# Value products of the samples in four column tiles, forget sums in four column tiles, and the samples' spatial weights turned once by VectorE

## The chip, the cores and the metric

One core of a Trainium2 chip runs the whole kernel. The metric is the time of one execution on the device in microseconds (us); less is better. The engines of the core each run their own instructions in order: TensorE (PE, with its weight loads listed apart as PEld), VectorE (DVE), ScalarE (ACT), GpSimd (POOL), and SyncE (SP), which issues most of the DMAs. They wait for one another through semaphores.

## What is computed

A trunk of two layers, for a prompt of 512 frames and eight samples of 16 frames each, 640 rows in all, with 1024 model channels, all in float32. Layer 0 mixes by spatial gating in blocks of 128 frames; layer 1 is attention with forget gates, over 16 heads of 128 channels. Each layer ends with an output product, two norms and a gated embedding. The parts that the change touches:

```python
# layer 0: a 128x128 matrix of spatial weights per group of 128 channels;
# samples use the first 16x16 of it (n = 16)
wm = jnp.where(chunk_causal_mask(n)[None], w_s[:, :n, :n], 0.0).astype(v.dtype)
s = jnp.einsum('gij,bnjgc->bnigc', wm, vb) + b_s[:, :n].T[None, None, :, :, None].astype(v.dtype)
# layer 1: running sums of the log forget values, and attention with them as a bias
cT = jnp.cumsum(logf, axis=1).transpose(0, 2, 1)
s = s + ci[..., :, None] - cT[:, :, None, :]
# layer 1, samples: 256 cached rows and 16 new ones
v = jnp.concatenate([v_cache.astype(v_new.dtype), v_new], axis=1)
p = jax.nn.softmax(s, axis=-1).astype(v.dtype)
return jnp.einsum('bhqk,bkhd->bqhd', p, v).reshape(B, T, H * dh)
```

## The kernel before, in words

**Products.** The large projections are made as three reduced-precision products of a high and a low part (`mm3`, L272 to L274). In both layers most of them run in a scheme of seven products instead of eight (`seven_products`): twelve matmuls of 128x320 for each of the seven, into four PSUM banks in turn (tiles named `pb`). ACT writes the high part of the weights (L289, L292) and DVE the low part (L290, L293); POOL makes the sums of weight blocks that the scheme wants (L211); DVE adds up the seven results (L713, L724, L726, L729). The small products are plain float32 matmuls, which leave two records each in the trace; transposes on PE leave one.

**Layer 0.** The groups of 128 channels are worked in pairs, eight pairs in all. Between the two projections of a pair, `spatial_weights` prepares two matrices for each of its groups. For the prompt it turns the 128x128 weights with PE (L688), and ACT copies them out with their mask (L690, L691). For the samples, DVE spreads the 16x16 weights along a block diagonal (L684) into the one buffer `ax`, PE turns that (L689), and ACT copies it out (L692). The 16x16 weights of all groups, `w16`, are gathered at the start of the layer by eight DMAs, one for each sample's 16 partitions. After the pair's projections, `gate_spatial` uses the matrices (L745 for the prompt, L746 for the samples). In the first three pairs a panel of layer norm is added (`layer_norm_panel`).

**Layer 1.** First the values, keys and queries of head pair 0 are projected. Meanwhile the logits of the forget gates are made in column tiles (L968: four matmuls with 32 output rows each, in four groups of 32 columns of PE), and from them the log forget values `lft`. `forget_sums` then makes the running sums for the prompt: four matmuls with the triangle of ones `tri`, for heads in 16 output rows and up to 512 columns (L1006). ACT copies them out, they are stored in `c_sc`, and `load_w0` reads one head's row back onto all 128 partitions when that head is due. The same routine makes the samples' sums (L1014 to L1016).

Then follow eight head pairs. For each, the projections of the next pair run on PE, and the attention of this pair is put between them: `interleave` gives each piece a time, and a scheduler turns the whole into an order for each engine. For the prompt a piece is scores, turn (transposes, L1186) or values (L1193). For the samples (`sample_pieces`, twice a pair, for four sequences each) the scores are eight matmuls of 32 output rows in column tiles (L1243). In `values`, one full-width matmul brings in the new rows of all four sequences (L1267), and eight of 32 output rows the cached ones (L1270), in four column groups. The last pair's attention stands between the output products of layer 1.

Of the kernel before, what the change touches and what calls it, by code (L numbers as in the profile page):

```python
# [17 lines left out]
F32 = mybir.dt.float32  # L18
# [39 lines left out]
def hybrid_trunk(tc, x_prompt, x_sample, ck, cv, clf, p_prompt, p_sample, norm_pre, norm_post,  # L58
# [27 lines left out]
    c_sc = dram.tile([H, SEQ], F32, name="c_sc")  # L86
# [579 lines left out]
    assert o_A + 256 <= o_X  # L666
    for b in range(NB):
        dma(w16[b * TS:(b + 1) * TS], w_s[0, :, :TS, :TS].rearrange("g i j -> i g j"))
# [11 lines left out]
    def spatial_weights(g):  # L680
        z = g % 2
        raw, wm, ws, ax = r1(o_wsr + z * P, P), r1(o_wm + z * P, P), r1(o_ws + z * P, P), r1(o_ax, P)
        nc.vector.scalar_tensor_tensor(out=spb[z], in0=spb[z], scalar=lnb[:, g:g + 1], in1=r1(o_bs + z * P, P), op0=ALU.mult, op1=ALU.add)
        nc.vector.tensor_tensor(  # L684
            out=ax.rearrange("p (b j) -> p b j", b=NB), in0=blk.rearrange("p (b j) -> p b j", b=NB),
            in1=w16[:, g:g + 1, :].broadcast_to([P, NB, TS]), op=ALU.mult)
        b = bank(SPA)
        nc.tensor.transpose(out=b[:, :P], in_=raw, identity=ident)  # L688
        nc.tensor.transpose(out=b[:, P:2 * P], in_=ax, identity=ident)  # L689
        nc.scalar.activation(out=wm[0:64, :], in_=b[0:64, 0:P], func=AF.Copy)  # L690
        nc.scalar.activation(out=wm[64:128, 64:128], in_=b[64:128, 64:P], func=AF.Copy)  # L691
        nc.scalar.activation(out=ws, in_=b[:, P:2 * P], func=AF.Copy)  # L692
# [263 lines left out]
    cT, ex, cS = r1(o_PT + 288, SEQ, H), r1(o_PT + 800, P), r1(o_V + 1760, 272)  # L956
# [46 lines left out]
    def forget_sums():  # L1003
        pb = bank(ATT)
        for t in range(4):
            nc.tensor.matmul(pb[:H, t * P:], lf3[:, t], tri[:, :SEQ - t * P], start=(t == 0), stop=(t == 3))  # L1006
        nc.scalar.activation(out=cT, in_=pb[:H, :], func=AF.Copy)
# [128 lines left out]
    def load_w0(h, queue=None):  # L1136
        dma(w0_of(h), c_sc[h].partition_broadcast(P), queue)
# [92 lines left out]
    def sample_pieces(p, bg):  # L1230
# [34 lines left out]
        def values():  # L1265
            O = bank(ATT)
            nc.tensor.matmul(O[:, :256], pt[:, 256:], v_of(p)[:, 4], start=True, stop=False)  # L1267
            for t in range(2):
                for bl in range(4):
                    nc.tensor.matmul(O[32 * bl:32 * bl + 32, :256], pt[:, t * P + 32 * bl:t * P + 32 * bl + 32],  # L1270
                                     vv[:, bl, t], start=False, stop=(t == 1))
# [136 lines left out]
```

## Time and profile before

| | |
|---|---|
| time, median of 3 runs | 1280.55 us (1275.15, 1280.55, 1281.59) |
| time of the profiled execution | 1274.95 us |
| its span, first to last instruction | 1273.1 us |
| mean granted clock of PE | 0.999 |
| layer 0, spatial pairs | about 127 to 345 us |
| forget sums | 566.2 to 568.5 us |
| attention of pairs 0 to 6 beside projections | about 581 to 1061 us |

The profile is that of one execution. Its page gives busy times, the chain of work that ended last, and groups of instructions by line. A row of a group has the line, the engine, the operation, what is written and read, the count, the busy time, the mean of one instruction, and the idle time before it with the engine that ended it. A row of the timeline has the start (us from the start of the span), the duration, the engine, line and operation, and how many records were merged into it. A row of the stages gives the busy time of PE, PEld, DVE, ACT and POOL in that order, each with its count, and then the granted clock, the DMA share and GB/s. Line numbers are those of the kernel before.

### The profile page before, as it was taken

The page shows a single profiled execution, that of the slowest core. Times are in us where ns is not written, and L with a number is a line of the kernel's source. Part 1 is how long each engine was busy: PE and PEld are TensorE (multiplying, and loading weights), DVE is VectorE, ACT ScalarE, POOL GpSimd, SP SyncE. Part 2 cuts the span into 40 slices and gives each one's busy share as a digit, 9 for nine tenths or more (in the row PEclk, how much of TensorE's full clock was granted, in tenths as well). Part 3 has the DMA queues.
Part 4 walks back from the last instruction along what each step waited for, and adds up shares of the span by engine and source line. Part 5 has one row for each costly group of instructions (what it writes and reads, how often), then busy time and mean ns, then how long its engine had stood idle before and what let it go on. Part 6 is the DMA issues. An engine that isn't in the chain of part 4 may idle for free.

```text
span 1273.1 us, 21241 instructions
## 1 busy us (share of the span) xinstructions
PE 1265.6 (99%) x7942; PEld 1138.3 (89%) x7942; DVE 957.5 (75%) x1795; ACT 595.3 (47%) x1076; POOL 353.3 (28%) x323
## 2 busy tenths in 40 slices
PE   9999999999999999999999999999999999999998
PEld 7888999999988888889999999999999999788887
DVE  6844999999943374799888898989888988545643
ACT  5424555444445253565445444545454545455331
POOL 1012445454000010155444434444435430000100
PEclk9999999999999999999999999999999999999999
DMA  5532343323324212658898758777888759632211
GB/s 204 177 102 67 112 125 120 92 88 98 121 85 161 88 35 87 150 125 174 159 169 169 185 150 187 164 164 143 152 162 179 178 114 287 221 129 83 67 66 50
DMA packets 275544, 171.52 MB, mean 135 GB/s; under 512 B 188721, under 2 KB 238689, under 8 KB 275442
## 3 DMA queue, kind: packets, MB, share of 16 engines
q1 hardware_dynamic: 261170, 127.80, 36.6%
q0 software_dynamic: 9760, 36.05, 14.0%
q10 hardware_dynamic: 4512, 6.33, 1.5%
q8 instruction: 62, 1.02, 0.3%
q14 instruction: 40, 0.33, 0.1%
HBM read 148.55 MB, written 21.59 MB: 134 GB/s over the span
## 4 chain that ended last, share of the span: by engine, by line
PE 98%; DVE 2%; DMA 0%; issue 0%; ACT 0%
PE pb L272 27%; PE pb L274 27%; PE pb L273 27%; PE pb L1193 3%; PE pb L419 2%; PE pb L1270 2%; PE pb L1186 1%; PE pb L1243 1%; PE pb L745 1%; PE pb L317 1%; PE pb L1058 1%; PE pb L1071 1%; PE pb L1267 1%; DVE W L290 0%; PE pb L1262 0%; PE pb L1059 0%
## 5 line engine op out<-in xcount | busy, mean ns | idle before, releaser
L272 PE MATMUL pb<-A,W 128*128 128x320 f32 (+1 forms) x752 | 240.8, 320 | 0.0
L273 PE MATMUL pb<-A,W 128*128 128x320 f32 (+1 forms) x752 | 233.8, 311 | 0.0
L274 PE MATMUL pb<-A,W 128*128 128x320 f32 (+1 forms) x752 | 233.3, 310 | 0.0
L290 DVE TENSOR_TENSOR W<-RAW,W 128x1024 fp32r<-128x1024 f32 (+1 forms) x122 | 146.1, 1198 | 73.0 <-ACT W L289 71.0
L273 PE MATMUL pb<-W,A 128*128 128x512 f32 x498 | 194.6, 391 | 0.0
L272 PE MATMUL pb<-W,A 128*128 128x512 f32 x498 | 194.6, 393 | 0.0
L274 PE MATMUL pb<-W,A 128*128 128x512 f32 x498 | 193.8, 392 | 0.0
L289 ACT ACTIVATE W<-RAW 128x1024 fp32r<-128x1024 f32 (+1 forms) x122 | 115.8, 949 | 87.9 <-PE pb L274 43.0
L272 PEld LDWEIGHTS pb<-A,W 128*128 128x128 f32 x752 | 141.7, 188 | 1.0 <-issue 0.2
L273 PEld LDWEIGHTS pb<-A,W 128*128 128x128 f32 x752 | 141.7, 188 | 0.5
L274 PEld LDWEIGHTS pb<-A,W 128*128 128x128 f32 x752 | 141.2, 188 | 0.0
L272 PE MATMUL pb<-tbf,W 128*128 128x320 f32 x360 | 119.0, 330 | 0.4 <-DVE R L1099 0.4
L303 POOL TENSOR_TENSOR SML<-SML 128x1 f32<-128x1 f32 x20 | 15.5, 777 | 349.8 <-DVE SML L301 345.0
L274 PE MATMUL pb<-tbf,W 128*128 128x320 f32 x360 | 111.4, 309 | 0.0
L273 PE MATMUL pb<-tbf,W 128*128 128x320 f32 x360 | 111.2, 309 | 0.0
L274 PEld LDWEIGHTS pb<-W,A 128*128 128x128 f32 x498 | 93.4, 188 | 19.3 <-issue 0.4
L273 PEld LDWEIGHTS pb<-W,A 128*128 128x128 f32 x498 | 93.6, 188 | 18.8
L272 PEld LDWEIGHTS pb<-W,A 128*128 128x128 f32 x498 | 93.5, 188 | 18.6
L211 POOL TENSOR_TENSOR sff<-RAW 128x512 f32<-128x512 f32 x46 | 60.9, 1324 | 177.4 <-DVE W L290 114.6
L713 DVE TENSOR_TENSOR R<-R,pb 128x320 f32<-128x320 f32 x184 | 86.5, 478 | 15.0 <-PE pb L274 13.7
L290 DVE TENSOR_TENSOR A<-R,A 128x640 fp32r<-128x640 f32 (+1 forms) x42 | 35.5, 880 | 57.6 <-ACT A L289 57.2
L272 PEld LDWEIGHTS pb<-tbf,W 128*128 128x128 f32 x360 | 67.8, 188 | 10.4 <-issue 6.6
(272 smaller groups left out, 2848.6 us busy)
## 6 DMA issues: line engine op xcount, KB each, us to landing
RAW<-in_fox_w_in POOLq DMA_DIRECT2D x46, 512.0 KB, 7.1
RAW<-in_gmlp_w_in SPq DMA_DIRECT2D x40, 512.0 KB
R<-in_cache_fox_k SPq DMA_DIRECT2D x128, 128.0 KB
R<-in_cache_fox_v SPq DMA_DIRECT2D x32, 512.0 KB
RAW<-in_gmlp_w_out SPq DMA_DIRECT2D x16, 512.0 KB
RAW<-in_ple_w_gate SPq DMA_DIRECT2D x16, 512.0 KB
RAW<-in_fox_w_out SPq DMA_DIRECT2D x16, 512.0 KB
R<-in_fox_w_in POOLq DMA_DIRECT2D x14, 512.0 KB, 7.8
```

Source lines behind the costliest of these rows:

```text
L211: nc.gpsimd.tensor_tensor(out=o, in0=a, in1=b, op=op)
L272: nc.tensor.matmul(out, lh, rh, start=start, stop=False)
L273: nc.tensor.matmul(out, lh, rl, start=False, stop=False)
L274: nc.tensor.matmul(out, ll, rh, start=False, stop=stop)
L289: first = nc.scalar.activation(out=hi, in_=src, func=AF.Copy)
L290: nc.vector.tensor_tensor(out=lo, in0=src, in1=f(hi), op=ALU.subtract)
L303: behind["pool"] = nc.gpsimd.tensor_tensor(out=q, in0=t, in1=mhalf, op=ALU.pow)
L317: behind["pe"] = nc.tensor.transpose(out=b[:, j * P:(j + 1) * P], in_=src[:, (4 * c + j) * P:(4 * c + j + 1) * P], identity=ident)
L419: line[e] = make(*args, **kw)
L713: behind["dve"] = nc.vector.tensor_tensor(out=into(i, j), in0=a, in1=b, op=ALU.add)
L1193: nc.tensor.matmul(O[:, d], v[:, j, hh * P:(hh + 1) * P], pt[:, j * P:(j + 1) * P], start=(j == 0), stop=(j == i))
L1270: nc.tensor.matmul(O[32 * bl:32 * bl + 32, :256], pt[:, t * P + 32 * bl:t * P + 32 * bl + 32], vv[:, bl, t], start=False, stop=(t == 1))
```

## The change

Three edits.

1. The sixteen transposes of the samples' spatial weights on PE (L689) and their copies (L692) go. The 16x16 weights are gathered twice, side by side, as 32 rows and 32 columns per group (sixteen DMAs), DVE turns them all in one instruction in blocks of 32, and ACT copies one half out as `w16`. DVE spreads the turned weights straight into the buffer that `gate_spatial` reads, one of two.
2. The running sums are made by ten matmuls with 32 output rows and 128 columns, in four column groups, one for each 128 frames. They stand in `cT` and `c_sc` as 128 rows of 128, so that a head's sums are read back in four pieces.
3. In the samples' `values` the new rows' product is made by four matmuls of 32 output rows as well, ahead of the cached ones, and the order of all twelve is fixed.

```diff
@@ -83,7 +83,7 @@
     PB = [psum.tile([P, 512], F32, name=f"pb{i}") for i in range(8)]
     x_sc = dram.tile([NT, P, D], F32, name="x_sc")
     y_sc = dram.tile([H, P, TOK], F32, name="y_sc")
-    c_sc = dram.tile([H, SEQ], F32, name="c_sc")
+    c_sc = dram.tile([P, P], F32, name="c_sc")
     cs_sc = dram.tile([P, 272], F32, name="cs_sc")
     rs_sc = dram.tile([16, P], F32, name="rs_sc")
 
@@ -664,8 +664,13 @@
     o_wsr, o_wm, o_ws, o_bs, o_ax, o_A = (T + 2560 + z for z in (0, 256, 512, 768, 1024, 1152))
     w16 = r1(o_A, 256).rearrange("p (g j) -> p g j", g=16)
     assert o_A + 256 <= o_X
+    twice, turned_twice = r1(o_u, 512), r1(o_u + 512, 512)
     for b in range(NB):
-        dma(w16[b * TS:(b + 1) * TS], w_s[0, :, :TS, :TS].rearrange("g i j -> i g j"))
+        for z in range(2):
+            dma(twice.rearrange("p (g z j) -> z p g j", g=16, z=2)[z, b * TS:(b + 1) * TS], w_s[0, :, :TS, :TS].rearrange("g i j -> i g j"))
+    with queued("dve"):
+        nc.vector.transpose(out=turned_twice, in_=twice)
+    nc.scalar.activation(out=w16, in_=turned_twice.rearrange("p (g z i) -> p g z i", g=16, z=2)[:, :, 0], func=AF.Copy)
     for z in range(2):
         nc.gpsimd.memset(r1(o_wm + z * P, P)[64:128, 0:64], 0.0)
     SPA = (4, 5, 6, 7)
@@ -679,17 +684,15 @@
 
     def spatial_weights(g):
         z = g % 2
-        raw, wm, ws, ax = r1(o_wsr + z * P, P), r1(o_wm + z * P, P), r1(o_ws + z * P, P), r1(o_ax, P)
+        raw, wm, ws = r1(o_wsr + z * P, P), r1(o_wm + z * P, P), r1(o_ws + z * P, P)
         nc.vector.scalar_tensor_tensor(out=spb[z], in0=spb[z], scalar=lnb[:, g:g + 1], in1=r1(o_bs + z * P, P), op0=ALU.mult, op1=ALU.add)
         nc.vector.tensor_tensor(
-            out=ax.rearrange("p (b j) -> p b j", b=NB), in0=blk.rearrange("p (b j) -> p b j", b=NB),
+            out=ws.rearrange("p (b j) -> p b j", b=NB), in0=blk.rearrange("p (b j) -> p b j", b=NB),
             in1=w16[:, g:g + 1, :].broadcast_to([P, NB, TS]), op=ALU.mult)
         b = bank(SPA)
         nc.tensor.transpose(out=b[:, :P], in_=raw, identity=ident)
-        nc.tensor.transpose(out=b[:, P:2 * P], in_=ax, identity=ident)
         nc.scalar.activation(out=wm[0:64, :], in_=b[0:64, 0:P], func=AF.Copy)
         nc.scalar.activation(out=wm[64:128, 64:128], in_=b[64:128, 64:P], func=AF.Copy)
-        nc.scalar.activation(out=ws, in_=b[:, P:2 * P], func=AF.Copy)
 
     def uv_of(g):
         return r1(o_u + (g % 2) * TOK, TOK), r1(o_tz + (g % 2) * TOK, TOK)
@@ -953,7 +956,7 @@
     fx, fa, fe, fl, fu, lft = (r1(o_V + 1280 + z * n, n) for z in range(6))
     lf3 = lft.rearrange("p (t h) -> p t h", t=NT)
     fx3 = fx.rearrange("p (t h) -> p t h", t=NT)
-    cT, ex, cS = r1(o_PT + 288, SEQ, H), r1(o_PT + 800, P), r1(o_V + 1760, 272)
+    cT, ex, cS = r1(o_PT + 288, P), r1(o_PT + 800, P), r1(o_V + 1760, 272)
     assert o <= o_K and o_PT + 288 >= o_P + 1280 and o_PTs + 96 >= o_qp + 1280
 
     def whole(i, j):
@@ -1003,8 +1006,10 @@
     def forget_sums():
         pb = bank(ATT)
         for t in range(4):
-            nc.tensor.matmul(pb[:H, t * P:], lf3[:, t], tri[:, :SEQ - t * P], start=(t == 0), stop=(t == 3))
-        nc.scalar.activation(out=cT, in_=pb[:H, :], func=AF.Copy)
+            for g in range(t, 4):
+                nc.tensor.matmul(pb[32 * g:32 * g + 32, :P], lft[:, t * H:t * H + 32], tri[:, (g - t) * P:(g - t + 1) * P],
+                                 start=(t == 0), stop=(t == g))
+        nc.scalar.activation(out=cT, in_=pb[:, :P], func=AF.Copy)
         dma(c_sc, cT, nc.scalar)
         nc.vector.tensor_tensor(
             out=ex.rearrange("p (r b h) -> p r b h", r=NB, b=NB),
@@ -1134,7 +1139,7 @@
         return tri if h % 2 else SF[:, 2048:2560] if h < 14 else r1(o_raw, 512)
 
     def load_w0(h, queue=None):
-        dma(w0_of(h), c_sc[h].partition_broadcast(P), queue)
+        dma(w0_of(h).rearrange("p (g n) -> p g n", g=4), c_sc.rearrange("(g h) n -> h g n", g=4)[h].partition_broadcast(P), queue)
 
     def prompt_pieces(h):
 
@@ -1264,11 +1269,12 @@
 
         def values():
             O = bank(ATT)
-            nc.tensor.matmul(O[:, :256], pt[:, 256:], v_of(p)[:, 4], start=True, stop=False)
-            for t in range(2):
-                for bl in range(4):
-                    nc.tensor.matmul(O[32 * bl:32 * bl + 32, :256], pt[:, t * P + 32 * bl:t * P + 32 * bl + 32],
-                                     vv[:, bl, t], start=False, stop=(t == 1))
+            with ExitStack() as stack:
+                for t in (2, 0, 1):
+                    for bl in range(4):
+                        last = nc.tensor.matmul(O[32 * bl:32 * bl + 32, :256], pt[:, t * P + 32 * bl:t * P + 32 * bl + 32],
+                                                v_of(p)[:, 4] if t == 2 else vv[:, bl, t], start=t == 2, stop=t == 1)
+                        stack.enter_context(tc.issue_after(last.ins))
             nc.scalar.activation(out=os_, in_=O[:, :256], func=AF.Copy, scale=kept["ri"])
 
         def gate():
```

The scheduler orders the whole program anew. Three places on PE, as the built programs have them. A row has the line, the operation, what is written and read, and the shape of the output; x is the count. The new lines L1010, L1021, L1191 and L1248 are L1006 (new form), L1016, L1186 and L1243 of before, and L1275 stands for L1267 and L1270.

The first place is the samples' values of head pair 1, first four sequences, on PE. Before:

```order
L274 MATMUL pb_71<-A,W 128x320
L1267 MATMUL pb_74<-R_69 128x256
L1270 MATMUL pb_74<-R_69 32x256 x2
L1186 MATMUL pb_76<-CST,R_69 128x128 x2
L1270 MATMUL pb_74<-R_69 32x256 x6
L272 MATMUL pb_72<-tbf,W 128x320
```

Now:

```order
L274 MATMUL pb_71<-A,W 128x320
L1275 MATMUL pb_74<-R_69 32x256 x4
L1191 MATMUL pb_76<-CST,R_69 128x128 x2
L1275 MATMUL pb_74<-R_69 32x256 x8
L272 MATMUL pb_72<-tbf,W 128x320
```

The full-width product is gone, and the two transposes of the prompt's attention stand after four tiles, where they stood after two. Pairs 2 to 6 read alike; in pair 0 the split is 3 and 9. For the other four sequences of a pair nothing stands between, before or now.

The second place is the forget sums on PE, between two projection products of the queries. Before:

```order
L274 MATMUL pb_72<-tbf,W 128x320
L1006 MATMUL pb_74<-CST,R_69 16x512
L1006 MATMUL pb_74<-CST,R_69 16x384
L1006 MATMUL pb_74<-CST,R_69 16x256
L1006 MATMUL pb_74<-CST,R_69 16x128
L272 MATMUL pb_73<-A,W 128x320
L1016 MATMUL pb_75<-CST,R_69 128x16
L273 MATMUL pb_73<-A,W 128x320
```

Now:

```order
L274 MATMUL pb_72<-tbf,W 128x320
L1010 MATMUL pb_74<-CST,R_69 32x128 x10
L1021 MATMUL pb_75<-CST,R_69 128x16
L272 MATMUL pb_73<-A,W 128x320
L273 MATMUL pb_73<-A,W 128x320
L274 MATMUL pb_73<-A,W 128x320
```

The last matmul of the samples' sums moved to just behind the prompt's. In what follows, the product into `pb_71` stands whole ahead of the one into `pb_70`; before, two of its twelve matmuls did.

The third place is the samples' first scores (pair 0, first four sequences) on PE. Before, eight together:

```order
L274 MATMUL pb_72<-A,W 128x320
L1243 MATMUL pb_74<-R_69 32x272 x8
L272 MATMUL pb_73<-tbf,W 128x320
L273 MATMUL pb_73<-tbf,W 128x320
L274 MATMUL pb_73<-tbf,W 128x320
```

Now, the first two of them, one product earlier:

```order
L272 MATMUL pb_71<-tbf,W 128x320
L273 MATMUL pb_71<-tbf,W 128x320
L274 MATMUL pb_71<-tbf,W 128x320
L1248 MATMUL pb_74<-R_69 32x272 x2
L272 MATMUL pb_72<-A,W 128x320
L273 MATMUL pb_72<-A,W 128x320
L274 MATMUL pb_72<-A,W 128x320
```

The other six stand where the eight stood, behind the product into `pb_72`.

## Prediction

> **What bounds the kernel now.** I read the page first, for the engine that is busy, then the waits of TensorE (PE), then the timeline of PE at each edited place, and last the busy time of VectorE (DVE) in the stages around those places.
>
> ```profile
> span 1273.1 us, 21241 instructions
> PE 1265.6 (99%) x7942; PEld 1138.3 (89%) x7942; DVE 957.5 (75%) x1795; ACT 595.3 (47%) x1076; POOL 353.3 (28%) x323
> PE 98%; DVE 2%; DMA 0%; issue 0%; ACT 0%
> ```
>
> PE is busy for 99% of the span and holds 98% of the chain that ended last. Its own waits behind the start-up are two:
>
> ```profile
> PE pb L272 <- DVE R L1099: 0.4, 1, 0.4
> PE pb L272 <- DVE R L726: 0.2, 1, 0.2
> ```
>
> So a microsecond less in PE's own stream is a microsecond less in the end, unless DVE, which follows PE, becomes late. I therefore count PE's issue intervals, from the start of one instruction to the start of the next. "Busy" won't do, because matmuls overlap. How near DVE is to PE:
>
> ```profile
> 127.00:139.70 12.70, 12.70 (x89) 12.69 (x89) 11.88 (x18) 6.31 (x11) 8.11 (x6) 1.00 0.45 152
> 167.40:195.20 27.80, 27.65 (x195) 27.38 (x194) 27.11 (x41) 15.59 (x29) 12.95 (x8) 1.00 0.40 122
> 565.00:581.00 16.00, 15.57 (x97) 13.45 (x97) 15.78 (x24) 7.67 (x13) 8.83 (x7) 1.00 0.79 156
> ```
>
> The third number behind the length is DVE's: 27.11 of 27.80 us in a pair of spatial groups, 15.78 of 16.00 us around the forget sums. These are the two places where a saving on PE may be handed back.
>
> **The value products.** One set for head pair 1, first four sequences, and one set for the other four:
>
> ```profile
> 667.13 0.31 PE L274 MATMUL pb<-A,W 128*128 128x320 f32 x1
> 667.28 0.59 PE L1267 MATMUL pb<-R 128*128 128x256 f32 x2
> 667.81 0.63 PE L1270 MATMUL pb<-R 128*32 128x256 f32 x4
> 668.36 0.44 PE L1186 MATMUL pb<-CST,R 128*128 128x128 f32 x2
> 668.73 1.06 PE L1270 MATMUL pb<-R 128*32 128x256 f32 x12
> 669.72 0.41 PE L272 MATMUL pb<-tbf,W 128*128 128x320 f32 x1
> ...
> 699.61 0.59 PE L1267 MATMUL pb<-R 128*128 128x256 f32 x2
> 700.13 1.07 PE L1270 MATMUL pb<-R 128*32 128x256 f32 x16
> 701.13 0.41 PE L272 MATMUL pb<-tbf,W 128*128 128x320 f32 x1
> ```
>
> Each of these products leaves two records, so x4 is two tiles and x16 is eight. Two tiles alone take 668.36 - 667.81 = 0.55 us, six take 669.72 - 668.73 = 0.99, eight take 1.00. So tiles on different column groups already run side by side: the cost goes by rounds of up to four, 0.55 for the first with its change of mode at the end and about 0.44 for each further one (six and eight tiles are both two rounds). The full-width L1267 takes 0.53 ahead of them.
>
> In the second set the full product (0.53) plus two rounds (1.00) become three rounds: 1.00 + 0.44 = 1.44, plus what entering the tiles costs straight from a projection product. That entry is in the sample scores:
>
> ```profile
> 583.84 0.31 PE L274 MATMUL pb<-A,W 128*128 128x320 f32 x1
> 584.08 1.12 PE L1243 MATMUL pb<-R 128*32 128x272 f32 x16
> 585.13 0.42 PE L272 MATMUL pb<-tbf,W 128*128 128x320 f32 x1
> ```
>
> 0.24 instead of the usual 0.15 us, so 0.09 more. 1.53 against 1.53: **nothing** is gained there. In the first set the two transposes of L1186 stand between, and they now come after four tiles, not after two. Before: 0.53 + 0.55 + 0.37 + 0.99 = 2.44. After: 0.09 + about 0.56 (one full round) + 0.37 + 1.00 = 2.02. **0.42 us** is won, because a broken round is gone. The built program has this 4 and 8 split for head pairs 1 to 6; pair 0 has 3 and 9 (four rounds, as before) and pair 7 has no break. So 6 x 0.42 = **2.5 us**.
>
> A rule speaks against it. The Trainium skill (TensorE: Matmul & The Clock Gate, "Measured speedup vs the span model") gives three column tiles a measured speedup of 2.38 and not 3. By it a packed round would cost 3 / 2.38 = 1.26 of a full product, an estimate, and the 16 packed rounds that take the place of full products would each be that much dearer. The trace doesn't agree: six tiles (a full and a half-filled round) and eight (two full ones) take 0.99 and 1.00.
>
> **The spatial weights.** 16 transposes leave PE:
>
> ```profile
> 139.66 0.31 PE L274 MATMUL pb<-A,W 128*128 128x320 f32 x1
> 139.81 0.27 PE L689 MATMUL pb<-CST,R 128*128 128x128 f32 x1
> 139.84 0.39 PE L272 MATMUL pb<-A,W 128*128 128x320 f32 x1
> 140.07 0.31 PE L273 MATMUL pb<-A,W 128*128 128x320 f32 x1
> ```
>
> L689 holds PE for 0.03, and the product behind it takes 0.23 instead of 0.15: 0.11 us each, **1.76 us** for 16. Of that, 0.11 in each of the three pairs with a layer-norm panel (DVE at 27.11 of 27.80) may be lost in a wait of PE for DVE's L726:
>
> ```profile
> 161.26 0.31 PE L274 MATMUL pb<-A,W 128*128 128x320 f32 x1
> 161.72 0.42 PE L272 MATMUL pb<-tb,W 128*128 128x320 f32 x1 [0.16 <-DVE R L726]
> ```
>
> 0.46 instead of 0.15, and the same some 28 us later, twice. If PE comes 0.11 earlier and DVE does not, the wait grows by it, 0.33 in all. Against it DVE itself gets shorter. L684 builds the spread weights:
>
> ```profile
> L684 DVE TENSOR_TENSOR R<-CST,R x16: 277/985/1402, 137.1 to 332.5; 128x128 f32<-128x128 f32 x16
> ```
>
> It has two buffers now instead of one, and the second of a pair moves up to just behind the first; at its fastest it takes 0.28 against a median of 0.99 us, so up to 0.7 us of DVE per pair may go, and the waits with it (three of 0.31). I take 0 for both, and keep +0.33 and -0.9 as ends.
>
> Added on DVE is one turn of 128x512. The nearest row:
>
> ```profile
> L1085 DVE STREAM_TRANSPOSE R<-R x16: 830/831/837, 560.0 to 1042.2; 128x640 f32<-128x640 f32 x16
> ```
>
> 0.83 x 512/640 = 0.67 us, once, ahead of the splits of the first pair's weights and of all that DVE has queued behind it. In 127 to 139.7 us DVE has 0.82 us idle and PE doesn't wait, so I take 0; without that cover it costs 0.67. ScalarE (ACT) loses 16 copies and gains one, and at 47% busy it sets nothing. SyncE issues 16 gathers instead of 8:
>
> ```profile
> 62.30 1.82 SPq L124 DMA_DIRECT2D R<-in_gmlp_w_s  x4
> 64.47 0.39 SPq L124 DMA_DIRECT2D RAW<-in_gmlp_w_in  x1
> ...
> 82.76 1.06 ACT L289 ACTIVATE W<-RAW 128x1024 fp32r<-128x1024 f32 x1 [4.01 <-issue]
> ```
>
> Four take 1.82, so eight more hold its queue 3.6 us longer, with weight loads among them. The ACT row is the split of the weight load in the second row, 18 us after its issue; PE waits nowhere there. I take 0; with the cover gone it is at most 3.6. The turn needs these bytes only at 125 us.
>
> **The forget sums.**
>
> ```profile
> 565.99 0.31 PE L274 MATMUL pb<-tbf,W 128*128 128x320 f32 x1
> 566.23 2.33 PE L1006 MATMUL pb<-CST,R 128*16 128x512 f32 x8
> 568.49 0.41 PE L272 MATMUL pb<-A,W 128*128 128x320 f32 x1
> 568.74 0.29 PE L1016 MATMUL pb<-CST,R 128*128 128x16 f32 x2
> 569.07 0.41 PE L273 MATMUL pb<-A,W 128*128 128x320 f32 x1
> 569.32 0.30 PE L274 MATMUL pb<-A,W 128*128 128x320 f32 x1
> ...
> 547.21 0.64 PE L968 MATMUL pb<-R,WF 128*32 128x128 f32 x16
> 547.78 0.33 PE L985 MATMUL pb<-CST,R 128*128 128x128 f32 x1
> ```
>
> Before: 568.49 - 566.23 = 2.26 us. After: ten tiles of 128 columns on groups 0123, 123, 23, 3, four rounds. The forget logits' eight tiles (L968) are two rounds of the same width in 0.57; two more at 2 x 0.11 each (the transpose's step for 128 columns) make 1.01. That wins 1.25, and L1016 now stands right behind the tiles, which spares one change of mode (0.25 - 0.15): **1.35 us**. Behind it PE waits for the bank that L1099 frees (the first wait above). The new order puts a whole product of twelve ahead of that wait instead of two, so PE still meets DVE at about the same time, having done 10 x 0.15 = 1.5 us more; the gain survives. If DVE, full there, holds PE at the next bank too, up to 1.35 is lost. The table of sums is now read in four pieces of 512 bytes per row instead of one of 2 KB, two heads ahead of use: 0.
>
> The same reordering **splits the first sample scores** (pair 0) into two tiles, a product, and six tiles. By the rows of L1243 (eight tiles 1.05) and the values' two tiles, widened from 256 to 272 columns (0.58), this is 0.09 + 0.58 + 0.10 and 0.09 + 1.04 + 0.10 instead of 0.09 + 1.05 + 0.10: **0.76 us lost**, once.
>
> **Sum.** 2.5 + 1.76 + 1.35 - 0.76 = 4.85 us less. The profiled execution took 1274.95 us, 1.85 around its span: 1270.1. The median of the runs is 1280.55 (1275.15, 1280.55, 1281.59), 5.6 above the profiled one, and I apply the sum to it: **1275.7 us**, 0.38% less. Ends of the unknown terms: -6.2 (the three DVE waits and the remainder of the 0.4 us wait vanish) and -1.8 (0.33, 0.67, 1.35 and about 0.7 of badly filled rounds lost).
>
> **Rivals.**
> - DVE takes the saving back. For it: 27.11 of 27.80 and 15.78 of 16.00. Against: outside three short waits PE never waits, and DVE's work shrinks. It would leave 2.5 - 0.76 = 1.7 us: 1278.8. Chance 0.12.
> - The packed rounds are dearer than I count: each costs 0.55, what the two tiles alone take, and not 0.44. For it: a third round in a row stands nowhere in the trace. Against: the eight tiles' second round. 16 x 0.11 = 1.8 us back, 1277.5. Chance 0.05. The rule of the Trainium skill quoted above (TensorE: Matmul & The Clock Gate) points this way.
> - **Slower:** in the new first round of the values four tiles stream the same rows of the new value block at once. L1243 and L1270 before stream different rows in each tile, so no row shows this. If PE serves them one after the other, each of the 16 sets costs three more of 0.44: +21 us, 1297. It decides against the change as soon as more than 0.3 us a set is lost. Chance 0.04.
> - The change doesn't do what it says: tiles ran side by side before, and only the broken rounds are won. That is in the sum already; if the profiler's order of issue misled me and the 4 and 8 split wins nothing, 2.4 us remain: 1278.2. Chance 0.06.
> - The forecast: 0.73. Within it the runs can fall at the lower of the two levels above, 1275.15 - 4.85 = 1270.3, about one time in three.
>
> From these: a measurement of this kernel tells about 0.5%, 6.4 us, from no change. Faster by more: the lower level, or the waits gone too, 0.31. Slower by more: 0.04 and 0.01 for a late gather. Same: 0.64. The range reaches from the lower level with some of the -6.2, 1269, to the upper run less the smallest gain, 1281.6 - 1.8 = 1279.8.
>
> **What would show it.** Right: no L689; value sets of 2.03 us with the L1186 pair after four tiles, 1.53 without; forget sums of 1.0 us; two score groups in pair 0. PE's waits for DVE not above 2 us in all. Wrong: a round of the new value block above 0.5 us, new waits of L272 on DVE between 127 and 230 or behind 571 us, or a wait for the 16 gathers.

## The result, and the profile after

| | before | after |
|---|---|---|
| time, median of 6 runs each | 1277.70 us (1275.11 to 1281.59) | 1293.05 us (1286.54 to 1301.30) |
| ratio, with its 95% interval | | 1.0131 (1.0107 to 1.0155) |
| profiled execution | 1274.95 us | 1291.54 us |
| its span, and mean granted clock | 1273.1 us, 0.999 | 1289.6 us, 0.996 |

The changed kernel is slower by 1.3%; 0.4% faster was predicted. Runs of the kernel before fall near 1275.5 or near 1280 us, in shares that differ from one set of runs to the next, so each ratio below is against the runs of before made beside it, and medians of different sets are not compared.

The head of the page of after:

```profile
span 1289.6 us, 21437 instructions
PE 1268.1 (98%) x8034; PEld 1138.6 (88%) x8034; DVE 958.2 (74%) x1796; ACT 592.6 (46%) x1061; POOL 354.4 (27%) x323
```

No engine's busy time grew by more than 2.5 us, and the span grew by 16.5. So the loss is time in which PE stands, or runs at a lower clock. The view of PE's waits names most of it (us in all, times, longest). Behind the start-up, before has only the two of 0.4 and 0.2 us that the prediction shows. L727 is L724 of before, for which PE doesn't wait there, and L729 is L726:

```profile
PE pb L272 <- DVE SML L1177: 5.3, 1, 5.3
PE pb L1191 <- DVE R L1185: 4.5, 3, 2.1
...
PE pb L272 <- DVE R L727: 1.3, 2, 0.7
PE pb L273 <- DVE A L290: 1.2, 1, 1.2
```

**The edits themselves.** The timeline of PE at the two value sets of head pair 1, and at the forget sums:

```profile
676.05 0.31 PE L274 MATMUL pb<-A,W 128*128 128x320 f32 x1
676.29 0.64 PE L1275 MATMUL pb<-R 128*32 128x256 f32 x8
676.86 0.44 PE L1191 MATMUL pb<-CST,R 128*128 128x128 f32 x2
677.23 1.07 PE L1275 MATMUL pb<-R 128*32 128x256 f32 x16
678.23 0.41 PE L272 MATMUL pb<-tbf,W 128*128 128x320 f32 x1
...
708.90 0.31 PE L274 MATMUL pb<-A,W 128*128 128x320 f32 x1
709.14 1.50 PE L1275 MATMUL pb<-R 128*32 128x256 f32 x24
710.57 0.41 PE L272 MATMUL pb<-tbf,W 128*128 128x320 f32 x1
```

```profile
567.08 1.08 PE L1010 MATMUL pb<-CST,R 128*32 128x128 f32 x20
568.09 0.40 PE L1021 MATMUL pb<-CST,R 128*128 128x16 f32 x2
568.33 0.39 PE L272 MATMUL pb<-A,W 128*128 128x320 f32 x1
569.92 0.41 PE L273 MATMUL pb<-A,W 128*128 128x320 f32 x1 [1.20 <-DVE A L290]
```

From the L274 to the L272 the first set takes 2.18 us (2.59 before), so 0.41 is won where 0.42 was forecast; the second takes 1.67, as before. The forget sums take 568.09 - 567.08 = 1.01 us, as forecast. But one product later PE waits 1.20 us for DVE's split of the activations, and of the 1.35 about 0.65 is left at 575 us (start of the same products on PE, before against after).

**The largest gap.** PE's timeline around 600 us, and DVE's:

```profile
597.33 0.31 PE L272 MATMUL pb<-tbf,W 128*128 128x320 f32 x1
602.94 0.69 PE L272 MATMUL pb<-W 128*128 128x384 f32 x1 [5.30 <-DVE SML L1177]
...
605.13 0.47 PE L274 MATMUL pb<-A,W 128*128 128x320 f32 x1
605.40 0.47 PE L272 MATMUL pb<-A,W 128*128 128x320 f32 x1
```

```profile
599.06 1.42 DVE L1224 STREAM_TRANSPOSE R<-R 128x256 f32<-128x256 f32 x4 [3.80 <-DMA R<-in_cache_fox_k]
```

Read from below: DVE stands 3.8 us for a load of cached keys that it has to turn. Queued behind it are the prompt's softmax (L1177, for which PE waits) and more. PE starts nothing for 5.6 us (5.3 of them idle), and afterwards a product's step is 605.40 - 605.13 = 0.27 instead of 0.147 us. The stages show why (length, busy PE, PEld, DVE, ACT, POOL, then the granted clock, DMA share and GB/s):

```profile
597.30:602.90 5.60, 0.34 (x3) 0.08 (x1) 3.84 (x12) 0.19 (x1) 1.01 (x1) 0.80 0.42 85
602.90:606.00 3.10, 3.06 (x11) 3.06 (x12) 3.10 (x5) 1.99 (x6) 2.94 (x3) 0.50 0.56 87
```

The granted clock is 0.50 behind the gap: the gap is paid for a second time. By the starts of the same products, after is 0.96 us behind before at 585 us and 8.91 behind at 605. Up to 1055 us another 4.9 are lost, in smaller waits and one more stretch at half the clock (net of the 2.5 that the values win there), and the rest in the last pair.

**Which transfers were late.** Where the key loads stand in the queue of SyncE, before and then after (start of the issue, length with its waits):

```profile
574.12 4.77 SPq L124 DMA_DIRECT2D out<-R  x4
579.00 0.40 SPq L124 DMA_DIRECT2D R<-in_cache_fox_v  x1
583.07 1.86 SPq L124 DMA_DIRECT2D out<-R  x4
585.03 14.22 SPq L124 DMA_DIRECT2D R<-in_cache_fox_k  x8
```

```profile
575.00 0.33 SPq L124 DMA_DIRECT2D out<-R  x1
575.50 1.98 SPq L124 DMA_DIRECT2D R<-in_cache_fox_v  x1
577.53 10.56 SPq L124 DMA_DIRECT2D out<-R  x7
588.19 2.33 SPq L124 DMA_DIRECT2D R<-in_cache_fox_k  x4
```

Two things differ. The value load has passed three of the four stores of new keys ahead of it, and the key load starts 3.2 us later. By the code, the value load could move up because its buffer is also scratch of the forget sums (`cS`, at `o_V`), and PE now finishes these earlier; on GpSimd a weight load moved ahead of one of the L211 sums. And each read of a head's row of `c_sc` is slower. The DMA views of 2 us of before and 4 us of after, at the first such read (the second line of each: packets, MB, share of the 16 engines' time):

```profile
DMA packets 201, 0.38 MB, mean 188 GB/s; under 512 B 15, under 2 KB 20, under 8 KB 201
q10 hardware_dynamic: 201, 0.38, 58.2%
```

```profile
DMA packets 322, 0.16 MB, mean 41 GB/s; under 512 B 0, under 2 KB 322, under 8 KB 322
q10 hardware_dynamic: 322, 0.16, 27.4%
```

The row for all partitions is 256 KB. It comes at 188 GB/s before, at 41 after, and in these stretches nothing else moves. By the packets in the traces, the first read takes 1.5 us from its first packet to its last before and 6.6 after. The fourteen reads that ACT issues take 1.5 to 7.0 us before (median 3.1), since most share the engines with other transfers, and 5.4 to 8.4 after (median 7.1). A weight load that GpSimd issues at 572.3 us before and 573.2 after brings its first packets at 574.4 and 578.8 us: in after it comes only when the first read, which ends at 579.5, is nearly done.

### The profile page after: what moved, and what is told of

The parts are those of the page before. It is cut to its first block, busy times and chain, and to the rows that moved or that the text cites. A ratio compares the mean times of both kernels' runs of the same rounds, so it can differ in the third digit from the quotient of the medians.

```text
span 1289.6 us, 21437 instructions
## 1 busy us (share of the span) xinstructions
PE 1268.1 (98%) x8034; PEld 1138.6 (88%) x8034; DVE 958.2 (74%) x1796; ACT 592.6 (46%) x1061; POOL 354.4 (27%) x323
## 3 DMA queue, kind: packets, MB, share of 16 engines
q0 software_dynamic: 9760, 36.05, 12.6%
## 5 line engine op out<-in xcount | busy, mean ns | idle before, releaser
L272 PE MATMUL pb<-A,W 128*128 128x320 f32 (+1 forms) x752 | 240.9, 320 | 1.3 <-DVE R L727 1.3
L274 PE MATMUL pb<-A,W 128*128 128x320 f32 (+1 forms) x752 | 233.3, 310 | 0.0
L290 DVE TENSOR_TENSOR W<-RAW,W 128x1024 fp32r<-128x1024 f32 (+1 forms) x122 | 151.2, 1240 | 70.6 <-ACT W L289 68.8
L272 PE MATMUL pb<-W,A 128*128 128x512 f32 x498 | 195.1, 394 | 0.6 <-ACT A L289 0.5
L274 PE MATMUL pb<-W,A 128*128 128x512 f32 x498 | 194.4, 392 | 0.0
L272 PEld LDWEIGHTS pb<-A,W 128*128 128x128 f32 x752 | 142.2, 189 | 3.1 <-DVE R L727 1.8
L274 PEld LDWEIGHTS pb<-A,W 128*128 128x128 f32 x752 | 141.6, 188 | 0.0
L272 PE MATMUL pb<-tbf,W 128*128 128x320 f32 x360 | 119.3, 331 | 0.0
L274 PE MATMUL pb<-tbf,W 128*128 128x320 f32 x360 | 111.8, 311 | 0.0
L272 PEld LDWEIGHTS pb<-W,A 128*128 128x128 f32 x498 | 93.6, 188 | 20.0 <-ACT A L289 0.9
L274 PEld LDWEIGHTS pb<-W,A 128*128 128x128 f32 x498 | 93.4, 188 | 19.7 <-issue 0.4
L211 POOL TENSOR_TENSOR sff<-RAW 128x512 f32<-128x512 f32 x46 | 61.1, 1329 | 177.8 <-DVE W L290 74.5
L290 DVE TENSOR_TENSOR A<-R,A 128x640 fp32r<-128x640 f32 (+1 forms) x42 | 35.5, 880 | 59.4 <-ACT A L289 59.4
L272 PEld LDWEIGHTS pb<-tbf,W 128*128 128x128 f32 x360 | 68.0, 189 | 9.8 <-issue 5.8
```

The lines of the kernel that those rows point to most:

```text
L211: nc.gpsimd.tensor_tensor(out=o, in0=a, in1=b, op=op)
L272: nc.tensor.matmul(out, lh, rh, start=start, stop=False)
L274: nc.tensor.matmul(out, ll, rh, start=False, stop=stop)
L290: nc.vector.tensor_tensor(out=lo, in0=src, in1=f(hi), op=ALU.subtract)
```

## Experiments

Three questions: is it the forget edit, and what about its table; what of the moved transfers; and is each edit alone worth what was forecast. In the expectations, theory A is the number of pieces of a read, B the new order of PE's work, D the distance of the pieces in memory, E that the distance is a power of two, R the order of the key load and what stands ahead of it. Diffs are cut to their core.

### One part alone, or left out

**e1_pieces**: before, with a row read in four pieces that lie 640 bytes apart.

```diff
-    c_sc = dram.tile([H, SEQ], F32, name="c_sc")
+    c_sc = dram.tile([H, 4, 160], F32, name="c_sc")
...
-        dma(w0_of(h), c_sc[h].partition_broadcast(P), queue)
+        dma(w0_of(h).rearrange("p (g n) -> p g n", g=4), c_sc[h][:, :P].partition_broadcast(P), queue)
```

> The kernel before, with one thing of the change: the table of running sums lies in DRAM so that each of the 16 reads of a row is made in four pieces of 512 bytes and not in one of 2 KB; no instruction of PE or DVE moves. Theory A (the pieces: one read takes about 7 us of the DMA queues instead of 1.3 to 5, the transfers behind it land late, DVE waits for them and PE for DVE): slower by 10 to 17 us, 1288 to 1295 us, with PE waits of several us behind 581 us. Theory B (the new order of PE's work brings the waits): within 2 us of the kernel before, 1276 to 1280 us.

Measured: ratio 1.0027 (1.0009 to 1.0045); the profiled execution 1275.3 us, without a gap. So four pieces of 512 bytes in place of one of 2 KB aren't most of the loss. The ratio leaves them 0.1 to 0.45%, and this trace doesn't show where. The first read takes 1.7 us from first packet to last; its DMA view:

```profile
DMA packets 723, 0.36 MB, mean 182 GB/s; under 512 B 13, under 2 KB 723, under 8 KB 723
```

**e2_rows**: after, with the table stored as rows of 512 and read whole.

```diff
-        dma(c_sc, cT, nc.scalar)
+        for g in range(4):
+            dma(c_sc[:, g * P:(g + 1) * P], cT[32 * g:32 * g + H], nc.scalar)
...
-        dma(w0_of(h).rearrange("p (g n) -> p g n", g=4), c_sc.rearrange("(g h) n -> h g n", g=4)[h].partition_broadcast(P), queue)
+        dma(w0_of(h), c_sc[h].partition_broadcast(P), queue)
```

> The changed kernel with all its edits on PE and DVE, but the table of running sums written to DRAM in four parts so that a row lies whole, and read in one piece of 2 KB as before. Theory A: the loss behind 581 us goes, 1274 to 1279 us, reads of a row drained in 1.3 to 5 us again and PE's waits behind 581 us under 2 us. Theory B: no change against the changed kernel, 1290 to 1296 us. The three more writes cost at most 1.2 us (3 x 0.38 us of issue on ACT).

Measured: 1281.28 us, ratio 1.0039 (1.0026 to 1.0052). Most of the loss is gone, but a gap of 6.3 us at 596 us stays: so there is a second cause.

**e3_noforget** and **e4_forget**: after without the forget edit (sums, table and reads as before), and before with it alone. The core of e3; e4 is the same the other way round:

```diff
-            for g in range(t, 4):
-                nc.tensor.matmul(pb[32 * g:32 * g + 32, :P], lft[:, t * H:t * H + 32], tri[:, (g - t) * P:(g - t + 1) * P],
-                                 start=(t == 0), stop=(t == g))
+            nc.tensor.matmul(pb[:H, t * P:], lf3[:, t], tri[:, :SEQ - t * P], start=(t == 0), stop=(t == 3))
```

> The changed kernel with the forget sums and the table as before; the values side by side and the turned spatial weights stay. Theory A: 1273 to 1279 us. Theory B, that the values' new order or the spatial turn carries the loss: 1285 us or more. In both the waits of PE for L727 near 190 and 219 us (about 1 us each in the changed kernel) stay, since they lie ahead of the forget sums.

> The kernel before with the forget sums side by side and the table in its new layout, without the other two edits. Theory A: 1287 to 1296 us, about as slow as the changed kernel. Theory B, that values or spatial turn carry the loss: 1275 to 1279 us.

Measured: 1.0003 (0.9989 to 1.0018) without it, 1.0123 (1.0106 to 1.0140) with it alone, there with a gap of 7.4 us at 597.7 us. The forget edit carries nearly all of the net loss; what e3 leaves near nothing is a gain and a loss of the other two edits (below).

### How far apart the pieces lie

**e5_far**: before, pieces 16 KB apart. **e17_far8**: 8 KB apart, with `[4, H, P]`, since H is 16. **e10_odd**: after, with the table padded from 32 to 33 rows a group, so that pieces lie 16.5 KB apart and not 16. The diffs of e5 and e10:

```diff
-    c_sc = dram.tile([H, SEQ], F32, name="c_sc")
+    c_sc = dram.tile([4, 32, P], F32, name="c_sc")
```

```diff
-    c_sc = dram.tile([P, P], F32, name="c_sc")
+    c_sc = dram.tile([4, 33, P], F32, name="c_sc")
```

> The kernel before, its table of running sums laid out as in the changed kernel: the four pieces of 512 bytes of a row lie 16 KB apart (in e1_pieces 640 bytes apart). No instruction of PE or DVE moves. Theory D (the distance: the reads of a row drain slowly because their pieces lie 16 KB apart): each read takes about 7 us and the kernel is slower by 6 to 14 us, 1282 to 1290 us, with PE waits of 1 to 3 us spread over 581 to 1110 us. Theory A (the number of pieces): as e1_pieces, reads in 1.5 to 4 us undisturbed, 1276 to 1280 us.

> The changed kernel with its table padded: the four pieces of a row lie 16.5 KB apart (33 rows of 512 bytes) and not 16 KB. Nothing else moves. Theory E (a distance of a power of two sends all pieces to one place of the memory): the reads of a row drain in 1.5 to 4 us as in e1_pieces, and the time falls from 1293 to 1279 to 1283 us, as in e2_rows. Theory F (pieces far apart are slow at any distance): reads of 7 us and 1290 to 1296 us as the changed kernel.

> e5_far with the four pieces of a row 8 KB apart instead of 16 KB. If any power of two this large sends the pieces to one place of the memory: reads of about 7 us undisturbed and 1283 to 1291 us as e5_far. If the place depends on 16 KB: reads of 1.5 to 4 us undisturbed and 1276 to 1280 us as e1_pieces; in between, half the pieces each at two places: 3.5 to 4 us.

Measured: e5 1.0092 (1.0070 to 1.0113), e17 1.0106 (1.0091 to 1.0122), e10 1.0025 (1.0011 to 1.0040). The DMA views at the first read in e17 and in e10:

```profile
DMA packets 299, 0.15 MB, mean 38 GB/s; under 512 B 0, under 2 KB 299, under 8 KB 299
```

```profile
DMA packets 746, 0.74 MB, mean 186 GB/s; under 512 B 24, under 2 KB 662, under 8 KB 746
q10 hardware_dynamic: 662, 0.40, 35.3%
```

In e10 the queue of the reads brings 0.40 MB in these 4 us, with 0.34 MB of weights beside it; in after 0.16, with nothing beside it. The first read takes 2.0 us from first packet to last in e10, 6.0 in e5 and 6.2 in e17. The same four pieces of 512 bytes are slow at 8 and 16 KB and not at 640 bytes or 16.5 KB. So it isn't the number, nor the distance as such: at the two powers of two tried, the read drains at about 40 GB/s. What in the memory makes it so no run here shows, and no other distances were run. In e10 PE's second wait of after is nearly gone too (4.5, 3 times, before the padding):

```profile
PE pb L1191 <- DVE R L1185: 0.6, 1, 0.6
```

### The moved transfers

**e6_vback**: e2 with the value load behind four of the eight stores again. **e7_keys_before**: before, with the key load ahead of the last four stores. **e8_together**: both at once on e2: the value load behind four stores, the other four behind the key load. The core of e6; in e7 and e8 `late_outs` follows `load_k(0, 1, 0)` and makes the last stores:

```diff
+        for qd in range(4):
+            if mid and qd == 2:
+                mid(out)
...
+    def first_v(out):
+        with queued("sp"):
+            load_v(0, 0, (1,))
+        rest.append(out)
```

> e2_rows with one DMA moved back: the second half of the first value cache load stands behind four stores of the new keys on SP's queue, as in the kernel before, and not behind one or two. Theory V (the load that moved ahead delays the stores' landing, so the next key load is issued 1.4 us later, meets the weight loads of POOL's queue and ends behind them): the key load is issued near 585.3 us instead of 586.4, the 6.3 us gap of PE near 596 us falls to at most 3.3 us, 1273 to 1278.5 us. Rival (PE's new order near 582 us, the split score group above all, makes the gap): the gap stays at 5 us or more, 1280 to 1283 us.

> The kernel before with one change of SP's order: the last four stores of the second head's new keys come behind the key load of pair 0 that is needed at 590 us, which stands ahead of them. Theory R (the two levels of the kernel before, 1275.2 and about 1280, are this key load ending just ahead of the weight loads or behind them): the load is issued 2 to 5 us earlier, ends by 586 us, and all runs lie at the lower level, 1274 to 1276.5 us. Rival (the levels have another cause, the chip's or the start's): the runs spread over 1275 to 1281 as before.

> All three edits of the change, the table read in whole rows (as in e2_rows), the value load behind four stores (as in e6_vback) and the key load ahead of the last four stores (as in e7_keys_before). If the two transfers are all that the change lost, what PE saves stays: values 2.5 us, forget sums about 0.7, spatial turn about 0.3 less than nothing: 1271 to 1273.5 us. If another wait takes their place: 1275 us or more.

Measured: 1.0038 (1.0025 to 1.0051), 1.0026 (1.0017 to 1.0036) and 1.0027 (1.0016 to 1.0038). All three missed what I hoped for. In e6 the gap stays at 5.8 us. PE keeps its new order there, as the rival wants it; but e16 below keeps it too and has no such gap. In e7 the first key load stands ahead of the stores but is issued at 585.1 us, no earlier than the 585.0 of before, and the next only at 596.9 instead of 592.7 (gaps of 1.1 and 2.7 us); so theory R isn't tested as meant and stays open. In e8 DVE waits 4.3 us for the late stores instead, and PE has a gap of 4.0 us. The value load's place alone is not the cause.

**e9_weights_later**: e6, and GpSimd's weight load behind the fourth sum of L211 again.

```diff
+            late = S2 + 4 <= state["raw"] < S3
+            with queued(*["sums"] * (state["raw"] == S2 + 11)):
...
+                    behind["sums"] = nc.gpsimd.tensor_tensor(out=o, in0=a, in1=b, op=op)
```

> e6_vback with one DMA of POOL moved: a weight load of 512 KB (into the block R) that the change brought ahead of POOL's last sum of four stands behind that sum again, as in the kernel before; PE, DVE, ACT and SP keep e6_vback's order. Theory W (this load starts 0.85 us earlier than before and its packets get ahead of the last pieces of the key load that DVE's turn needs at 590 us): the load is issued at 587.3 us or later instead of 586.1, the key load's packets end by 590 us, the 5.8 us gap of PE near 596 us is at most 1 us; some 3 us may come back at the next key load, so 1273 to 1278 us. Rival (the transfers of 581 to 605 us are too many in any order, since stores, keys and weights have fixed needs): 1279 us or more, the gap only moves.

Measured: 1.0009 (0.9996 to 1.0022); the gap falls from 5.8 us to two of 1.7 and 2.5. PE, DVE, ACT and SyncE do the same in the same order as in e6, so the weight load's place alone is worth about 0.3% here; the time is still above what theory W said.

**e13_nostore** (on e10) and **e14_nostore_before** (on before) leave out the stores of head 1's new keys; that head's rows are then missing from the two cache outputs.

```diff
-        for qd in range(4):
+        for qd in range(4 if h != 1 else 0):
```

> e10_odd without the eight stores of the second head's new keys between 574 and 589 us (that head's new keys are left out of the two cache outputs); every compute engine keeps its order. Theory T (stores, value and key loads and weight loads of 571 to 605 us get in each other's way, and the key load that DVE turns lands late): without the stores the key load starts before 583 us, PE has no gap above 1 us between 581 and 610 us, and the time falls from 1281.4 to 1273 to 1276 us. Rival (PE's or DVE's own new order makes the gap): 1279 us or more, with the gap.

> The kernel before without the same eight stores (that head's new keys are left out of the two cache outputs). By theory T nearly all its runs lie at its lower level, 1274 to 1276 us, and e13_nostore is 0 to 3 us below it: what the change is worth when no transfer is late. If the levels of the kernel before have another cause, its runs spread over 1275 to 1281 us.

Measured: 1.0010 (1.0001 to 1.0019) and 1.0022 (1.0007 to 1.0036). Both missed: 1277.27 and 1279.25 us in the median. In e13 the key load is issued at 578.5 us and the gap at 597 us is gone, but one of 1.9 us opens at 600.3; in e14, where less is done than in before, the weight loads run 1.6 us later and a gap of 2.7 us opens at 600.5. So it isn't simply a matter of how much there is to store.

**e15_nospatial**: e10 without the spatial edit. **e16_dmas_back**: e15 with both transfers put back (the edits of e6 and e9).

> The change without the spatial weights' edit, its table padded as in e10_odd: values and forget sums stay. If the spatial edit is what sets off the late key load (e12_spatial, all ten runs at 1280 us or more): 1271.5 to 1274 us, the fastest of all. If the forget sums' moved DMAs do it on their own (the gaps of e4_forget at 597 us): 1277 to 1280 us.

> e15_nospatial with the two moved DMAs back: the value load behind four stores (as in e6_vback) and the weight load behind POOL's fourth sum (as in e9_weights_later). Values and forget sums stay, the spatial edit is out, the table is padded. If the order of these two loads sets off the gap of e15_nospatial at 596 us (4.1 us of waits): the gap falls under 1.5 us and the time to 1272 to 1275 us. If the stretch of 571 to 605 us has no slack in any order (e7, e12 and e14 had gaps with the order of the kernel before): 1276 to 1280 us.

Measured: e15 1.0024 (1.0013 to 1.0034), with a gap of 3.1 us at 596.4; e16 0.9986 (0.9976 to 0.9995), 1273.83 us, its largest gap behind 571 us 1.1 us. PE, DVE and ACT do the same in the same order in both. The value load is issued at 574.8 us in e15 and at 578.6 in e16. The weight load and PE's longest wait in that stage, in e15 and then in e16:

```profile
585.41 0.77 POOL L122 DMA_DIRECT2D R<-in_fox_w_in  x1
PE pb L272 <- DVE SML L1174: 2.8, 1, 2.8
```

```profile
586.84 0.77 POOL L122 DMA_DIRECT2D R<-in_fox_w_in  x1
PE pb L1209 <- DVE R L1203: 0.7, 1, 0.7
```

The stage from 571 to 605 us of before, after and e16 (columns as above):

```profile
571.00:605.00 34.00, 33.61 (x240) 30.88 (x239) 30.98 (x70) 17.74 (x33) 18.72 (x19) 1.00 0.83 170
```

```profile
571.00:605.00 34.00, 28.70 (x192) 26.73 (x191) 25.31 (x53) 13.93 (x25) 15.93 (x17) 0.94 0.72 150
```

```profile
571.00:605.00 34.00, 33.30 (x239) 30.06 (x239) 31.38 (x67) 17.27 (x32) 18.32 (x18) 1.00 0.82 167
```

PE does 240, 192 and 239 matmuls in the same 34 us. With both transfers back, 0.38% (4.9 us) comes back, with PE's new order as it was: the two moved DMAs are the second cause. Of the two it is mainly the weight load: the value load's place gives nothing between e2 and e6 (1.0039 and 1.0038), the weight load's 0.3% between e6 and e9. With the spatial edit in place, as in e9, the two together don't make the stage clean.

### The other two edits

**e11_values** is before with the values' edit alone, **e12_spatial** before with the spatial edit alone, **e18_gathers** before with only its eight extra gathers, into a buffer that nothing reads. The line added in e18:

```diff
+        dma(r1(o_u, 256).rearrange("p (g j) -> p g j", g=16)[b * TS:(b + 1) * TS], w_s[0, :, :TS, :TS].rearrange("g i j -> i g j"))
```

> The kernel before with the values' edit alone. By the sum of the prediction 2.5 us less, six steps of 0.42 us at head pairs 1 to 6: 1272 to 1274 us. If the wait of 3.2 us near 601 us that e3_noforget shows comes with this edit: 1275 to 1277 us.

> The kernel before with the spatial weights' edit alone. By the sum of the prediction 1.76 us less, 1273.5 to 1275 us. By the traces of e2_rows and e3_noforget, where PE waits 0.6 us for L727 at 188 and 216 us and comes out about 0.3 us later at 345 us: 1275.5 to 1276.5 us; slower than that if the wait near 601 us comes with this edit.

> The kernel before with nothing of the change but the eight more gathers of 64-byte pieces on SP's queue near 62 to 67 us (their bytes go where nothing reads them). Theory G (the eight gathers, 500 us earlier, shift the place of every later transfer in its queue, and that alone makes the stores of 574 to 584 us land about 1 us later, as in e12_spatial): PE shows gaps of 1 to 3 us between 590 and 607 us and the runs lie at 1278 to 1282 us. Rival (PE's or DVE's timing after the spatial edit does it): as the kernel before, median 1275 to 1276.5 us, no gap.

Measured: e11 0.9971 (0.9954 to 0.9988), 1274.21 us, which beats both kernels; between 599 and 995 us PE goes from 0.19 us behind before (its start-up) to 2.33 ahead, six steps of 0.42. In this program pair 0 has the 4 and 8 split too, and a seventh step follows at 1006 us; 0.8 is lost again in the last pair. e12 1.0042 (1.0028 to 1.0056), **slower** by 5.4 us. e18 1.0006 (0.9990 to 1.0022): not told from before.

Why the spatial edit loses shows only in part. DVE's groups by form, from 127 to 345 us, before (L684, L290) and after (L689 in place of L684):

```profile
L684 DVE TENSOR_TENSOR R<-CST,R 128x128 f32<-128x128 f32 x16 | 12.6, 785 | 0.0
...
L290 DVE TENSOR_TENSOR W<-R,W 128x512 fp32r<-128x512 f32 x7 | 4.8, 683 | 0.0
```

```profile
L290 DVE TENSOR_TENSOR W<-R,W 128x512 fp32r<-128x512 f32 x7 | 9.5, 1363 | 2.7 <-ACT W L289 2.7
L689 DVE TENSOR_TENSOR R<-CST,R 128x128 f32<-128x128 f32 x16 | 7.8, 488 | 0.0
```

The spreading gets shorter by 12.6 - 7.8 = 4.8 us, and the weight split L290 longer by 4.7. In before each of the seven splits lies beside a sum of POOL for 0.52 us and takes 0.68. In after three lie beside it for 1.18 and take 1.72, and three for 0.68 to 0.69 and take 1.23. At 187 us DVE comes to L727 1.2 us later, and PE waits for L727 twice. In the spatial stage 1.76 is won on PE and about 2 lost in such waits: over it, by the starts of the same products, after falls 0.3 us further behind. The rest of e12's loss lies at 596 and 601 us (gaps of 1.2 and 2.7 us), in the stage of the key loads, 250 us behind the edit (and one of 2.5 at 947). Why this edit alone makes them is left open; e18 doesn't settle it.

## Why the prediction was wrong

- **Values**: right, in mechanism and size: 0.41 in the first set of pair 1, nothing in the second, and steps of 0.42 in e11. In after some of it is covered by the waits for L1185, which fall between the tiles of such sets. Alone it gives 0.9971, within its interval the forecast 2.5 us. The rival that the four tiles with the same rows are served one after the other falls: the twelve tiles take 1.43 us (709.14 to 710.57), 0.43 more than the eight of before, where one after the other they would take 1.3 longer still. So its 1297, which is near the measured time, is near it by chance.
- **Packed rounds dearer**: falls with the same rows. The rule of the Trainium skill named there (TensorE: Matmul & The Clock Gate, "Measured speedup vs the span model") is again not borne out: the third round adds 0.43, less than the full-width product's 0.53.
- **Forget sums**: 1.01 us, as forecast. Half of the 1.35 is handed back in a wait for DVE, as the lower end allowed; the row of DVE at 15.78 of 16.00 us had said so.
- **Score split**: 0.76 lost, as forecast.
- **The step that failed**: "The table of sums is now read in four pieces of 512 bytes per row instead of one of 2 KB, two heads ahead of use: 0". I priced how long a read has until its use, and took for granted that it takes as long as before. Undisturbed it takes 6.6 us instead of 1.5, and in the median 7.1 instead of 3.1, sixteen times, and it holds up what is queued with it. e5 and e17, which add nothing but this to before, give 1.0092 and 1.0106, 12 to 14 us (of which some 3 may be the number of pieces, by e1's 1.0027); e10, which takes nothing but this from after, gives 1.0025 where after gave 1.0131.
- **A step that is missing**: I read how PE's order changed and not the order on SyncE and GpSimd behind the forget edit. Two DMAs moved, and putting them back is worth 0.38% (e15 to e16), most of it by the weight load (e6 to e9). Behind a gap the clock was 0.50, which makes it larger.
- **Spatial weights**: 1.76 on PE, as forecast, but the term for DVE, costed at 0 with ends of +0.33 and -0.9, was mis-sized: about +2. I took the time that L684 loses as won for DVE; by the trace it was time beside a sum of POOL, and that now falls on L290.
- **"What would show it"** held: new waits of L272 on DVE between 127 and 230 and behind 571 us are what I had put down as the sign of a wrong forecast.

The parts, each by its own comparison: the table's layout 12 to 14 us, the two DMAs 5, the spatial edit 3 to 5 (e12 against before, e3 against e11, e9 against e16, though e10 against e15 shows nothing), the values -2.5 to -3.7. They overlap around 600 us and aren't to be added up closely; the whole is 16.6 in the profiled executions. With both causes taken back, e16 (0.9986) shows no gain over the values alone (e11, 0.9971): no run here shows the forget edit to be worth anything in the end, for the 0.65 us that are left of it are about the 0.76 that the split scores cost.

## What to carry to other kernels

When an edit changes the layout of something in DRAM, price the read by its own rate, and look at the distance between the pieces of one descriptor row: 33 rows in place of 32 took back some 12 us here. When an edit frees a buffer earlier, read the order of every queue that issues DMAs, not only that of the busiest engine: a load that moves up can make the one that is due next late (about 0.3% for one weight load here, e6 to e9). And where a neighbour slowed an instruction, removing that instruction may only hand the neighbour to the next one.

## What the runs showed that was not expected

- The first read of 4 x 512 bytes by 128 partitions, from first packet to last: 1.7 us with pieces 640 bytes apart and 2.0 at 16.5 KB, but 6.0 and 6.6 at 16 KB and 6.2 at 8 KB; as one row of 2 KB 1.5.
- The clock behind a gap. It falls to 0.50 at 600.6 us, within the gap from 597.3 to 602.9, and stays there for 6.8 us, 4.5 of them behind the gap. Two later gaps, in the values of the samples, differ in what follows (stages with PE alone: length, busy, clock, DMA share, GB/s):

```profile
600.70:607.40 6.70, 4.46 (x16) 0.50 0.50 78
745.30:747.70 2.40, 0.31 (x8) 1.00 0.10 14
747.80:751.20 3.40, 3.40 (x30) 1.00 0.97 223
815.40:817.50 2.10, 0.28 (x8) 1.00 0.00 0
817.60:819.00 1.40, 1.40 (x19) 1.00 0.15 20
819.10:822.40 3.30, 3.30 (x11) 0.50 0.88 175
```

  The shorter gap is followed, 1.4 us later, by some 3.4 us at 0.50, the longer by none. The Trainium skill (TensorE: Matmul & The Clock Gate, "Part 1: The HAM clock gate") has the clock halved after an idle window of about 3.4 us that runs freely. The lengths of 3.4 and 6.8 us agree with such windows, but by these rows less than a whole window without work can be enough. The trace shows why the two gaps differ: all changes of its clock between 600 and 823 us (600.6, 607.5, 819.1, 822.5) lie whole multiples of 3.41 us apart. On that grid the shorter gap, 1.91 us of idle time, lies within one step, and the longer, 2.14, is cut at 747.4 us and leaves 1.80 in the step before. Taking all kept traces from 127 to 1265 us, and each trace's own grid: behind a step at full clock with 1.91 us idle or more (thirteen) the clock was 0.50, and behind one with up to 1.85 it stayed at 1.00, but for a step of 1.69 (e17, 1078.5 us).
- Four tiles that stream the same rows run side by side like four with different rows: three rounds in 1.43 us, where two of the latter took 1.00.
